# Up and gate projections turned to activations-stationary, with down projections in two passes and taps summed four tiles at a time

## The chip, the cores and the metric

The kernel runs on one core of a Trainium2 chip. The metric is the device time of one execution in microseconds (us); lower is better. Engines are named TensorE (PE, its weight loads PEld), VectorE (DVE), ScalarE (ACT), GpSimd (POOL) and SyncE (SP, which issues most DMAs). Each engine works off its own instructions in the order in which they were written out; engines wait for each other by semaphores.

## The reference

Two post-norm layers over 256 positions of width 2048, in float32. The first layer mixes with a gated MLP over windows of 128 positions, the second with latent attention; each mixer is followed by a gated MLP with a causal convolution of width 3.

```python
def gmlp_mixer(x, w_in, ln_g, ln_b, w_s, b_s, w_out):
    z = jax.nn.gelu(x @ w_in)                 # 2048 -> 2 x 6144
    u, v = jnp.split(z, 2, axis=-1)
    v = layer_norm(v, ln_g, ln_b)
    ...
    s = jnp.einsum('gij,bnjgd->bnigd', w, v) + ...   # 8 groups, masked 128x128
    return (u * s.reshape(B, S, GM_HALF)) @ w_out

def conv_ffn(x, w_up, conv_w, conv_b, w_down):
    h = x @ w_up                              # 2048 -> 2 x 5504
    h = lax.conv_general_dilated(h, ...) + conv_b    # 3 taps along the positions, per channel
    a, g = jnp.split(h, 2, axis=-1)
    return (jax.nn.silu(g) * a) @ w_down

for i in range(DEPTH):
    m = gmlp_mixer(...) if i % 2 == 0 else mla_mixer(...)
    x = layer_norm(ALPHA * x + m, ...)
    f = conv_ffn(x, ...)
    x = layer_norm(ALPHA * x + f, ...)
```

## The kernel before

Every float32 product is made from rounded halves: an operand is split into `hi` (rounded to the type float32r) and `lo` (the rest), and hi x hi, hi x lo and lo x hi are accumulated. The split of a weight load is a cast on ScalarE (`wh<-raw`) and a subtraction on VectorE (`wl<-raw,wh`).

`Feed` (line 48) walks through all weights in the order of use, as loads of 128 x 2048 (1 MB) by SyncE. `next` hands out one load and sees that two more are split and another two loaded; a load is split in two halves of 1024 columns. All tiles of this size come from one pool, `big`.

There are two forms of product. `prod_b` (line 185) holds a 128 x 128 block of activations stationary in TensorE and streams 512 weight columns: 6 matmuls of 512 for each block of 128 rows and 512 columns of weights (3 products, 2 blocks of positions). The output has positions on the partitions. `prod_a` (line 196) holds a 128 x 128 block of weights and streams the activations, `hi` and `lo` side by side: a pair of matmuls of 512 and 256 columns. The output has channels on the partitions, and its two halves have to be added (`sum_halves`).

The stages in order: `v` (prod_b, 6 groups of 1024 columns), `u` (prod_a, 12 groups of 4 tiles, each tile followed by `gate`), `wo` (`down`, prod_b), boundary with the layer norm and the first 512 columns of the up projection (`upf`), `up` (prod_a, groups 1 to 21; each pair of tiles goes through `conv` and Silu in `pair`), `dn` (`down`), boundary (`mq`), latent attention (`mq`, `mkv`, `qr`, `qn`, `kn`, `sc`, `vv`, `mo`), boundary, the second `up` and `dn`, final norm.

`down` (line 217) keeps all 8 PSUM banks: 4 pieces of 512 columns for 2 blocks of positions, one load of weights (128 x 2048) a step. The last `SKEW` steps are held back and worked off piece by piece in `boundary`, so that the norm can begin. The residual stays in two tiles of `big`.

A scheduler sets the order on each engine when the kernel is built; what stands in the code is the order in which it takes the instructions up, and an instruction whose operands it holds ready may stand earlier.

Of the kernel before, what the change touches and what calls it, by code (L numbers as in the profile page):

```python
# [15 lines left out]
P = 128  # L16
# [19 lines left out]

# [6 lines left out]


SKEW = 3


class Feed:

    def __init__(self, nc, pool, chunks):
        self.nc, self.pool, self.chunks = nc, pool, chunks
        self.raw, self.parts = {}, {}
        self.loaded = self.split = self.used = 0

    def _load(self):
        ap, cols = self.chunks[self.loaded]
        t = self.pool.tile([P, 2048], F32, tag="big", name=f"raw{self.loaded}")
        step = 512 if self.loaded == 0 else cols  # L60
        for o in range(0, cols, step):
            self.nc.sync.dma_start(t[:, o : o + step], ap[:, o : o + step])
        self.raw[self.loaded] = t
        self.loaded += 1

    def _split(self):
        i = self.split
        cols = self.chunks[i][1]
        raw = self.raw.pop(i)
        hi = self.pool.tile([P, 2048], F32R, tag="big", name=f"wh{i}")  # L70
        lo = self.pool.tile([P, 2048], F32R, tag="big", name=f"wl{i}")
        step = 512 if i == 0 else 1024 if cols == 2048 else cols // 2
        for o in range(0, cols, step):
            c = slice(o, o + step)
            self.nc.scalar.copy(hi[:, c], raw[:, c])  # L75
            self.nc.vector.tensor_tensor(lo[:, c], raw[:, c], hi[:, c].bitcast(F32), ALU.subtract)  # L76
        self.parts[i] = (hi, lo)
        self.split += 1

    def ahead(self, n_load, n_split):  # L80
        while self.split < min(n_split, len(self.chunks)):
            if self.loaded == self.split:
                self._load()
            self._split()
        while self.loaded < min(n_load, len(self.chunks)):
            self._load()

    def next(self, splits=2, loads=2):
        i = self.used
        self.ahead(i + 1 + splits + loads, i + 1 + splits)  # L90
        self.used += 1
        return self.parts.pop(i)
# [3 lines left out]
def trunk(ctx: ExitStack, tc: tile.TileContext, x, xT, gm_in, gm_wout, ffn_up, ffn_dn,  # L96
# [4 lines left out]
    big = ctx.enter_context(tc.tile_pool(name="big", bufs=22))  # L101
    tp = ctx.enter_context(tc.tile_pool(name="tp", bufs=3))
    st = ctx.enter_context(tc.tile_pool(name="st", bufs=4))
    ps = ctx.enter_context(tc.tile_pool(name="ps", bufs=8, space=bass.MemoryType.PSUM))
# [32 lines left out]
    xhl = [slot([P, 4, 512], f"xhl0_{q}", F32R) for q in range(4)]  # L137
    for j in range(4):
        t = slot([P, 4, S], f"xraw{j}")
        parts = [slice(q, q + 1) for q in range(4)] if j == 0 else [slice(0, 2), slice(2, 4)]  # L140
# [39 lines left out]

# [14 lines left out]

# [5 lines left out]
    def sum_halves(acc, name):  # L201
        lo = tp.tile([P, S], F32, tag="t1", name=f"lo_{name}", bufs=8)
        nc.scalar.copy(lo, acc[:, S : 2 * S])
        h = tp.tile([P, S], F32, tag="t1", name=f"h_{name}", bufs=8)
        nc.vector.tensor_tensor(h, acc[:, 0:S], lo, ALU.add)
        return h

    def split_act(src, name):

        t = tp.tile([P, 2 * S], F32R, tag="t2", name=name, bufs=6)  # L210
        nc.scalar.copy(t[:, 0:S], src)
        nc.vector.tensor_tensor(t[:, S : 2 * S], src, t[:, 0:S].bitcast(F32), ALU.subtract)
        return t

    full = [(f * 512, 512) for f in range(4)]

    def down(n_k, get_src, tag, ln, skew=SKEW):

        acc = [[bank(f"{tag}_{b}_{f}") for f in range(4)] for b in range(2)]
        late = []  # L220
        a = {}
        for k in range(n_k):
            for j in range(k, min(k + 2, n_k)):
                if j not in a:
                    a[j] = split_act(get_src(j), f"{tag}a{j}")
            left = n_k - 1 - k
            hi, lo = feed.next(splits=2 if left > 8 else 3 if left > 3 else 4, loads=2 if left > 3 else 1)
            if left == 6:
                ln.prep()
            t = a.pop(k)  # L230
            if left < skew:
                late.append((t, hi, lo, k))
                continue
            for b in range(2):
                prod_b(acc[b], (t[:, b * P : (b + 1) * P], t[:, S + b * P : S + (b + 1) * P]),
# [614 lines left out]
```

## Time and profile before

| | |
|---|---|
| Median of 3 runs | 2559.76 us (2559.61 to 2564.33) |
| Span of the profiled execution | 2559.8 us (its own time is not given apart from the span; the median lies within 0.1 us of it) |
| Instructions | 32217, of which matmuls 13041 |
| Stage `v` | to 272.7 us |
| Stage `u` | 272.7 to 562.3 us |
| Stage `wo` | 562.3 to 825.0 us |
| First `up` | 849.7 to 1313.6 us |
| First `dn` | 1313.6 to 1549.2 us |
| Second `up` | 1851.2 to 2315.2 us |
| Second `dn` | from 2315.2 us; the last matmul begins at 2548.9 us |

Spans go from the first to the last instruction. A row of a group reads: line, engine, operation, output and inputs by name, shapes, count, then busy time in us, mean time of one in ns, idle time of the engine before it and who ended that. Matmul times overlap: a matmul of 512 columns has a duration of 0.39 us, while the next begins much earlier; so a rate is read from a stretch of time and the number of matmuls in it.

### The profile page before, as it was taken

How to read it: one execution, taken by the hardware profiler on the slowest of the kernel's cores; microseconds unless marked ns; L12 is line 12 of the kernel's file. 1: busy time of each engine (PE TensorE's matmuls, PEld its weight loads, DVE VectorE, ACT ScalarE, POOL GpSimd, SP SyncE). 2: the span in 40 equal slices, each digit the busy share in tenths (PEclk: the TensorE clock that was granted, in tenths of full speed). 3: DMA queues.
4: the chain of work that ended last, by engine and by line, in shares of the span. 5: the costliest groups of instructions: out<-in, count | busy, mean ns of one | idle time of the engine just before them, and what ended most of it. 6: DMA issues, size and time to landing. Idle time of an engine off the chain costs nothing.

```text
span 2559.8 us, 32217 instructions
## 1 busy us (share of the span) xinstructions
PE 2544.2 (99%) x13041; PEld 2152.4 (84%) x13041; DVE 1573.6 (61%) x2284; ACT 1226.4 (48%) x1795; POOL 2.4 (0%) x15
## 2 busy tenths in 40 slices
PE   9999999999999999999999999999999999999998
PEld 7888888888888888888888888877888888888886
DVE  6444675575546766665675547845676576667554
ACT  5434444455443555544554433544365455446441
POOL 0000000000000000000000000000000000000000
PEclk9999999999999999999999999999999999999999
DMA  8545454556563545544565554424555454446552
GB/s 323 194 165 197 165 181 165 181 211 230 200 231 148 214 173 188 182 171 175 198 222 205 205 203 159 165 99 154 191 198 181 163 199 174 184 169 242 206 205 87
DMA packets 68838, 480.18 MB, mean 188 GB/s; under 512 B 7633, under 2 KB 8273, under 8 KB 11729
## 3 DMA queue, kind: packets, MB, share of 16 engines
q1 hardware_dynamic: 68688, 478.13, 52.0%
q8 instruction: 102, 1.67, 0.3%
q14 instruction: 48, 0.39, 0.0%
HBM read 476.00 MB, written 2.10 MB: 187 GB/s over the span
## 4 chain that ended last, share of the span: by engine, by line
PE 99%; DVE 1%; DMA 0%; ACT 0%; issue 0%; SPq 0%; DVEq 0%; ACTq 0%
PE up L113 36%; PE dn L113 18%; PE u L113 10%; PE v L113 10%; PE wo L113 10%; PE mo L113 4%; PE upf L113 2%; PE sc L113 1%; PE mkv L113 1%; PE qn L113 1%; PE kn L113 1%; PE vv L113 1%; PE mq L113 1%; PE s L113 1%; PE qr L113 0%; PE lnt L366 0%
## 5 line engine op out<-in xcount | busy, mean ns | idle before, releaser
L76 DVE TENSOR_TENSOR wl<-raw,wh 128x1024 fp32r<-128x1024 f32 (+2 forms) x886 | 1050.6, 1214 | 473.3 <-ACT wh L75 294.1
L75 ACT CAST wh<-raw 128x1024 fp32r<-128x1024 f32 (+2 forms) x886 | 891.0, 1044 | 523.9 <-DVE wl L76 202.8
L113 PE MATMUL up<-xhl,wh 128*128 128x512 f32 x2624 | 927.5, 399 | 0.0
L113 PE MATMUL up<-xhl,wl 128*128 128x256 f32 x2624 | 737.6, 281 | 0.0
L113 PEld LDWEIGHTS up<-xhl,wh 128*128 128x128 f32 x2624 | 493.5, 188 | 122.6
L113 PEld LDWEIGHTS up<-xhl,wl 128*128 128x128 f32 x2624 | 496.5, 189 | 0.1
L113 PE MATMUL u<-xhl,wh 128*128 128x512 f32 x768 | 268.8, 397 | 0.0
L113 PE MATMUL u<-xhl,wl 128*128 128x256 f32 x768 | 212.2, 279 | 0.0
L113 PE MATMUL v<-wh,xhl 128*128 128x512 f32 x768 | 208.2, 392 | 1.8 <-ACT wh L75 1.8
L113 PE MATMUL wo<-wh,woa 128*128 128x512 f32 x768 | 194.5, 390 | 0.0
L113 PE MATMUL dn<-wh,dn1a 128*128 128x512 f32 x688 | 174.2, 389 | 0.0
L113 PE MATMUL dn<-wh,dn0a 128*128 128x512 f32 x688 | 173.5, 390 | 0.0
L113 PEld LDWEIGHTS v<-wh,xhl 128*128 128x128 f32 x768 | 145.1, 189 | 33.1 <-ACT wh L75 2.3
L113 PEld LDWEIGHTS u<-xhl,wh 128*128 128x128 f32 x768 | 143.5, 188 | 32.8
L113 PEld LDWEIGHTS wo<-wh,woa 128*128 128x128 f32 x768 | 144.1, 188 | 29.8
L113 PEld LDWEIGHTS dn<-wh,dn0a 128*128 128x128 f32 x688 | 129.1, 188 | 26.8
L113 PEld LDWEIGHTS dn<-wh,dn1a 128*128 128x128 f32 x688 | 129.1, 188 | 26.7
L113 PEld LDWEIGHTS u<-xhl,wl 128*128 128x128 f32 x768 | 144.7, 188 | 1.1
L113 PE MATMUL v<-wl,xhl 128*128 128x512 f32 x384 | 119.0, 391 | 0.0
L113 PE MATMUL wo<-wl,woa 128*128 128x512 f32 x384 | 107.0, 390 | 0.0
L113 PE MATMUL dn<-wl,dn1a 128*128 128x512 f32 x344 | 96.0, 389 | 0.0
L113 PE MATMUL dn<-wl,dn0a 128*128 128x512 f32 x344 | 95.2, 390 | 0.0
(204 smaller groups left out, 2113.5 us busy)
## 6 DMA issues: line engine op xcount, KB each, us to landing
raw<-in_ffn_up_dram SPq DMA_DIRECT2D x172, 1024.0 KB, 4.8
raw<-in_gm_in_dram SPq DMA_DIRECT2D x95, 1024.0 KB, 4.7
raw<-in_ffn_dn_dram SPq DMA_DIRECT2D x86, 1024.0 KB, 4.7
raw<-in_gm_wout_dram SPq DMA_DIRECT2D x48, 1024.0 KB, 4.8
raw<-in_ml_out_dram SPq DMA_DIRECT2D x16, 1024.0 KB, 4.8
raw<-in_ml_b_dram SPq DMA_DIRECT2D x14, 1024.0 KB, 4.9
raw<-in_ml_kv_dram SPq DMA_DIRECT2D x5, 864.0 KB, 4.7
lng<-in_ln_rows_dram SPq DMA_DIRECT2D x4, 1024.0 KB, 6.3
```

Source lines behind the costliest of these rows:

```text
L75: self.nc.scalar.copy(hi[:, c], raw[:, c])
L76: self.nc.vector.tensor_tensor(lo[:, c], raw[:, c], hi[:, c].bitcast(F32), ALU.subtract)
L113: nc.tensor.matmul(o, l, r, start=start, stop=stop, skip_group_check=True)
```

## The change

What it does:

- `u` and `up` go from `prod_a` to the form of `prod_b`. `Square` takes 1024 weight columns as 2 x 2 PSUM banks (2 blocks of positions, 2 pieces of 512), 8 loads of 24 matmuls a group. There are 6 groups of `u` (numbers 0 to 5) and 10 groups of `up` (0 to 9) in each layer, and a tail of 2 loads that keeps `prod_a`. `out` brings the four banks into SBUF on ScalarE (Gelu in `u`, a copy in `up`: `h0_1` is that of group 1 of the first layer), and TensorE transposes each 128 x 128 block (`uT`, `ht`).
- `turned` takes four transposed tiles at a time. `conv3` writes the three taps with ScalarE, 12 instructions of 256 columns (`c0` an Identity with scale and bias, `c1` and `c2` copies with a scale), and VectorE adds the shifted taps of all four in two additions. One Silu and one multiplication of 512 follow.
- `down` takes two passes over 1024 output columns each, the second in reverse order of the steps. Its activations are split four steps at a time by `split4`, in each pass. The last 3 loads of the second pass are held back.
- A load of `u`, `up`, `wo` and `dn` is two DMAs with rows of 4 KB. A load is split whole (2048 columns), not in halves. `Feed.next` counts the tiles of `big` (now 21, before 22) and stops short of `room`.
- The residual is written to DRAM after each boundary (`park`, DMAs issued by ScalarE) and read back (`residual`) before the next norm.
- `gate` becomes `gates`, two tiles at a time; its `sb` is scaled by ScalarE.

The code also has a form with 7 products for 8 blocks (`seven`). The tables that would choose it (`GROUP_V`, `GROUP_U`, `GROUP_UP`, `SEVEN_WO`, `SEVEN_DN`) name no step, so it makes no instruction.

```diff
-SKEW = 3
+BIG = 21
+LATE = 3
+MID = 4
+T2 = 4
...
     def _split(self):
...
-        step = 512 if i == 0 else 1024 if cols == 2048 else cols // 2
+        step = 512 if self.split == 0 else cols
         for o in range(0, cols, step):
             c = slice(o, o + step)
-            self.nc.scalar.copy(hi[:, c], raw[:, c])
-            self.nc.vector.tensor_tensor(lo[:, c], raw[:, c], hi[:, c].bitcast(F32), ALU.subtract)
+            nc.scalar.copy(s.hi[:, c], raw[:, c])
+            nc.vector.tensor_tensor(s.lo[:, c], raw[:, c], s.hi[:, c].bitcast(F32), ALU.subtract)
...
+    def wide(src, base, p, sv):
+        o = (p % 2) * 1024
+        return Step([(c * 1024, 1024, src[base + 4 * c + p // 2][:, o : o + 1024]) for c in range(2)], 2048,
+                    (2 * p, 2 * p + 1), False, sv)
...
+        def plain(self, s, xs, b, fs, last):
+            for j, k in enumerate(s.ks):
+                xh, xl = x_parts(xs, k, b)
+                for which, (a, w) in enumerate(((xh, s.hi), (xh, s.lo), (xl, s.hi))):
+                    for f in fs:
+                        mm(self.acc[b][f], a, w[:, s.at(j, f)], not self.begun[b][f], last and which == 2)
+                        self.begun[b][f] = True
...
+        def out(self, name, func=None):
+            z = slot([P, 4, 512], name) if self.e is None else self.e
+            for f in range(2):
+                for b in range(2):
+                    o, src = z[:, 2 * b + f], self.acc[b][f]
...
+                    if func is not None:
+                        nc.scalar.activation(o, src, func)
+                    elif self.e is None:
+                        nc.scalar.copy(o, src)
+            return z
...
-    def conv(layer, F, acc, name):
-        h = acc if acc.shape[-1] == S else sum_halves(acc, name)
-        w = C_CONV + (layer * 2 * NF_FF + F) * 4
-        c = tp.tile([P, S], F32, tag="t1", name=f"c_{name}", bufs=8)
-        nc.scalar.activation(c, h, AF.Identity, bias=cst[:, w + 3 : w + 4], scale=cst[:, w + 2 : w + 3])
-        nc.vector.scalar_tensor_tensor(c[:, 1:S], h[:, 0 : S - 1], cst[:, w + 1 : w + 2], c[:, 1:S],
-                                       ALU.mult, ALU.add)
-        nc.vector.scalar_tensor_tensor(c[:, 2:S], h[:, 0 : S - 2], cst[:, w : w + 1], c[:, 2:S],
-                                       ALU.mult, ALU.add)
-        return c
+    def conv3(layer, tiles, name):
+        n = len(tiles)
+        c = [tp.tile([P, 4, S], F32, tag="mid", name=f"c{i}_{name}", bufs=MID) for i in range(3)]
+        for i, (F, src) in enumerate(tiles):
+            w = C_CONV + (layer * 2 * NF_FF + F) * 4
+            nc.scalar.activation(c[0][:, i], src, AF.Identity, bias=cst[:, w + 3 : w + 4], scale=cst[:, w + 2 : w + 3])
+            nc.scalar.activation(c[1][:, i], src, AF.Copy, scale=cst[:, w + 1 : w + 2])
+            nc.scalar.activation(c[2][:, i], src, AF.Copy, scale=cst[:, w : w + 1])
+        y = c[0][:, 0:n]
+        nc.vector.tensor_tensor(y[:, :, 1:S], y[:, :, 1:S], c[1][:, 0:n, 0 : S - 1], ALU.add)
+        nc.vector.tensor_tensor(y[:, :, 2:S], y[:, :, 2:S], c[2][:, 0:n, 0 : S - 2], ALU.add)
+        return y
...
+        for g in range(10):
+            feed.room = BIG - 6 - len(sums) // 2 - (4 * g + 5) // 8
...
+            z = square(f"up{layer}_{g}", GROUP_UP[g], xhl, sums, f"h{layer}_{g}").out(f"h{layer}_{g}")
+            for f in range(2):
+                banks = [bank(f"ht{layer}_{g}_{f}_{i}") for i in range(2)]
+                for i in range(2):
+                    for j in range(2):
+                        for b in range(2):
+                            o = j * S + b * P
+                            q = i * 256 + j * P
+                            nc.tensor.transpose(banks[i][:, o : o + P], z[:, 2 * b + f, q : q + P], ident)
+                turned(2 + 4 * g + 2 * f, banks)
...
+        def park(self):
+            r = []
+            for b in range(2):
+                t = dram.tile([P, D], F32, name=f"parked{self.idx}_{b}")
+                nc.scalar.dma_start(t, self.res[b])
+                r.append(t)
+            return r
```

The order at three places. In the names, `wh166` is the cast half of load number 166; the loads of `up` group g in the first layer are 148 + 8g to 155 + 8g, those of the tail 228 and 229, and the down projection begins with 230.

ScalarE at the end of group 2 of `up` in the kernel before (its loads were numbered 152 to 155; `lo_0a4` empties half a bank, `c_0a4` is the Identity of `conv`):

```order
L203 COPY lo_0a4_6848<-up0_2_0_6684 128x256 [waits PE_49]
L75 CAST wh161_7010<-raw161_6936 128x1024 [waits DMAHW6_49,DVE_49]
L460 ACTIVATE c_0a4_6852<-h_0a4_6850,cst_187 128x256 [waits DVE_49]
L203 COPY lo_0g4_6856<-up0_2_2_6686 128x256 [waits PE_49]
L75 CAST wh161_7010<-raw161_6936 128x1024
L460 ACTIVATE c_0g4_6860<-h_0g4_6858,cst_187 128x256 [waits DVE_49]
L75 CAST wh162_7092<-raw162_6976 128x1024 [waits DMAHW7_49,DVE_49]
L476 ACTIVATE s0_4_6864<-c_0g4_6860 128x256 [waits DVE_49,Activation_49]
```

ScalarE after group 1 of `up` in the changed kernel, from the last cast ahead of the copies to the next one (left out are the other conv instructions; `s0_6` and `s0_8` are the Silus of the two calls of `turned`):

```order
L100 CAST wh165_6071<-raw165_6013 128x2048 [waits DMAHW6_49,DMAHW5_49,PE_49]
L410 COPY h0_1_6102<-up0_1_0_0_5850 128x512 [waits PE_49]
L410 COPY h0_1_6102<-up0_1_1_1_5853 128x512 [waits PE_49]
L701 ACTIVATE c0_0_6_6117<-ht0_1_0_0_6107,cst_177 128x256 [waits PE_49]
L702 ACTIVATE c1_0_6_6118<-ht0_1_0_0_6107,cst_177 128x256 [waits Activation_49]
L702 ACTIVATE c1_0_8_6148<-ht0_1_1_0_6137,cst_177 128x256 [waits DVE_49]
L717 ACTIVATE s0_6_6134<-c0_0_6_6117 128x512 [waits DVE_49]
L703 ACTIVATE c2_0_8_6149<-ht0_1_1_0_6137,cst_177 128x256 [waits Activation_49]
L717 ACTIVATE s0_8_6165<-c0_0_8_6147 128x512 [waits DVE_49]
L100 CAST wh166_6172<-raw166_6044 128x2048 [waits DMAHW7_49,DMAHW0_49]
```

Before, casts alternate with the small steps of the convolution. Now, after the odd groups, 24 conv instructions and two Silus stand between the casts of the second and the third load of the next group. After the even groups two casts more stand ahead of them:

```order
L410 COPY h0_2_6420<-up0_2_0_0_6168 128x512 [waits DVE_49,PE_49]
L410 COPY h0_2_6420<-up0_2_0_1_6169 128x512 [waits PE_49]
L100 CAST wh174_6489<-raw174_6362 128x2048 [waits DMAHW7_49,DMAHW0_49,DVE_49]
L410 COPY h0_2_6420<-up0_2_1_0_6170 128x512 [waits PE_49]
L410 COPY h0_2_6420<-up0_2_1_1_6171 128x512 [waits PE_49]
L100 CAST wh175_6520<-raw175_6393 128x2048 [waits DMAHW2_49,DMAHW1_49,DVE_49]
L701 ACTIVATE c0_0_10_6435<-ht0_2_0_0_6425,cst_177 128x256 [waits PE_49]
```

The third and fourth copy have moved behind a cast there, and the fourth load is cast before the first conv instruction.

TensorE at the same place, from the last matmul of group 2 (here seven matmuls of group 3 stand among the transposes; after the odd groups the 16 transposes stand together). Before, group 3 followed group 2 directly:

```order
L167 MATMUL up0_2_1_1_6171<-wh171_6327,xhl1_3_5282 128x512
L756 MATMUL ht0_2_0_0_6425<-ident_181,h0_2_6420 128x128 [waits Activation_49]
L756 MATMUL ht0_2_1_1_6456<-ident_181,h0_2_6420 128x128 [waits PE_49]
L167 MATMUL up0_3_0_0_6485<-wh172_6358,xhl1_0_5279 128x512
L167 MATMUL up0_3_0_0_6485<-wl172_6359,xhl1_0_5279 128x512 [waits DVE_49]
L756 MATMUL ht0_2_0_0_6425<-ident_181,h0_2_6420 128x128 [waits Activation_49]
L756 MATMUL ht0_2_1_0_6455<-ident_181,h0_2_6420 128x128 [waits Activation_49]
L167 MATMUL up0_3_1_0_6487<-wh172_6358,xhl1_0_5279 128x512
```

ScalarE at the end of the first `up` (`tl0_0` empties the tail's bank, `dn0a0_0` is the first cast of the down projection's activations; before, those casts stood among the casts of `up`, some groups earlier):

```order
L717 ACTIVATE s0_40_8703<-c0_0_40_8685 128x512 [waits DVE_49]
L770 COPY tl0_0_8786<-tl0_0_8706 128x256 [waits PE_49]
L100 CAST wh230_8708<-raw230_8582 128x2048 [waits DMAHW6_49,DMAHW5_49]
L770 COPY tl0_1_8789<-tl0_1_8707 128x256 [waits PE_49]
L100 CAST wh231_8747<-raw231_8613 128x2048 [waits DMAHW7_49,DMAHW0_49]
L701 ACTIVATE c0_0_t_8792<-tl0_0_8786,cst_177 128x256 [waits DVE_49]
L702 ACTIVATE c1_0_t_8793<-tl0_0_8786,cst_177 128x256 [waits Activation_49]
L703 ACTIVATE c2_0_t_8794<-tl0_0_8786,cst_177 128x256 [waits Activation_49]
L298 CAST dn0a0_0_8812<-act0_0_5526 128x4x256
```

The first activations of the down projection have moved behind the last conv chain and two casts of weights.

More of the change, by code (lines that the diff above doesn't have):

```diff
@@ L132, in trunk @@
+    steps += whole(ml_kv[5, :, 0:KVR], KVR)
+    for t in (ml_b, ml_out):
+        for i in range(t.shape[0]):
+            steps += whole(t[i])
+    steps += up_steps(1)
+    steps += back(ffn_dn[1], NF_FF, SEVEN_DN)
+    feed = Feed(nc, big, steps)
     idle = cpool.tile([P, 512], BF16, name="idle")
@@ L215, in trunk, with split4 @@
[L215 to L235, printed above, removed]
-                       hi, lo, full, k == 0, False)
+    def split4(src8, q, n, name):
+        t = slot([P, 4, 512], name, F32R)
+        t4 = t.rearrange("p (w k) c -> p w k c", k=2)
+        src = src8[:, 2 * (q % 2) : 2 * (q % 2) + 2]
+        for w, k in ((2, 2),) if n == 4 else ((n // 2, 2), (n // 2 + 1, 1)):
+            c = (slice(None), slice(0, w) if k == 2 else slice(w - 1, w), slice(0, k))
+            hi = t4[(*c, slice(0, S))]
+            nc.scalar.copy(hi, src[c])
+            nc.vector.tensor_tensor(t4[(*c, slice(S, 2 * S))], src[c], hi.bitcast(F32), ALU.subtract)
+        return t
@@ new lines, in trunk @@
+    for gi in range(6):
+        feed.room = BIG - 4 - len(seven_quads(GROUP_U)) - 7
+        gates(gi, square(f"u{gi}", GROUP_U[gi], xhl, sums, f"u{gi}"))
+    ln = Norm(0, [x[b * P : (b + 1) * P, :] for b in range(2)])
+    acc, end = down(NF_GM, pT, SEVEN_WO, "wo", ln)
+    def conv3(layer, tiles, name):
[10 more added lines that the diff above has]
+        return y
@@ new lines, in ffn @@
+        feed.room = BIG - 12
+        tail = [bank(f"tl{layer}_{f}") for f in range(2)]
+        for c in range(2):
+            hi, lo = feed.parts()
+            for j in range(8):
+                k = 8 * c + j
+                for f in range(2):
+                    o = j * 256 + f * P
+                    prod_a(tail[f], xhl, k, hi[:, o : o + P], lo[:, o : o + P], k == 0, k == KD - 1)
+        tiles = []
+        for f in range(2):
+            t = tp.tile([P, 2, S], F32, tag="t2", name=f"tl{layer}_{f}", bufs=T2)
+            nc.scalar.copy(t[:, 0], tail[f][:, S : 2 * S])
+            nc.vector.tensor_tensor(t[:, 1], tail[f][:, 0:S], t[:, 0], ALU.add)
+            tiles.append((f * NF_FF + NF_FF - 1, t[:, 1]))
@@ L516, in trunk @@
+        gated(NF_FF - 1, conv3(layer, tiles, f"{layer}_t"), 1)
+        ln = Norm(2 * layer + 1, parked, last)
+        return (ln, *down(NF_FF, act, SEVEN_DN, f"dn{layer}", ln))
+    ln, acc, end = ffn(0, ln, acc, end, False)
     cq = [slot([P, 4, 512], "cq", F32R)]
@@ L569, in after_q @@
             latent_put(b, 0, cq, C_QG)
-    boundary(ln, acc, end, range(4), "mq", after_q)
-    xhl, res = ln.new, ln.res
+    boundary(ln, acc, end, "mq", after_q)
+    xhl, parked = ln.new, ln.park()
     kvp = [(0, KVR // 2), (KVR // 2, KVR // 2)]
```

541 lines of the change are left out of this document (353 added, 188 removed).

## The prediction

> **What bounds the kernel now.** I read the page first, then who makes TensorE wait, then the busy times by stage. From the page, the engines' busy time and the shares of the chain that ended last:
>
> ```profile
> PE 2544.2 (99%) x13041; PEld 2152.4 (84%) x13041; DVE 1573.6 (61%) x2284; ACT 1226.4 (48%) x1795; POOL 2.4 (0%) x15
> PE 99%; DVE 1%; DMA 0%; ACT 0%; issue 0%; SPq 0%; DVEq 0%; ACTq 0%
> ```
>
> All waits of TensorE (total us, times, longest):
>
> ```profile
> PE v L113 <- ACT wh L75: 1.8, 1, 1.8
> PE o L113 <- ACT pts L681: 1.5, 1, 1.5
> PE warm L113 <- POOL idle L133: 1.3, 1, 1.3
> PE qn L113 <- ACT qnlo L636: 0.5, 1, 0.5
> ```
>
> TensorE waits 5.1 us in the whole program. So every matmul added or removed counts in full, and a wait that the change creates has nothing to be traded against. Busy time by stretch: steady `v` stage, `u` stage, the two `up` stages; then the 16 `s` matmuls of one group of `u` (columns: stretch, length, busy time and instructions of each engine, clock, DMA share, GB/s; the last row has PE alone):
>
> ```profile
> 50.00:250.00 200.00, 200.00 (x880) 164.97 (x879) 99.14 (x96) 85.46 (x98) 0.00 (x0) 1.00 0.54 193
> 272.70:562.30 289.60, 289.60 (x1730) 255.29 (x1728) 197.07 (x349) 136.92 (x205) 0.00 (x0) 1.00 0.51 179
> 849.70:1313.60 463.90, 463.90 (x2629) 402.49 (x2628) 305.52 (x457) 249.01 (x378) 0.00 (x0) 1.00 0.51 184
> 1851.20:2315.20 464.00, 464.00 (x2629) 402.73 (x2628) 305.58 (x457) 249.06 (x378) 0.00 (x0) 1.00 0.52 184
> 295.27:296.97 1.70, 1.70 (x16) 1.00 0.26 34
> ```
>
> The `v` stage already has the form that the change gives to `u` and `up`: activations stationary, 512 weight columns moving, 200.00/880 = 0.2273 us a matmul. A 128x128 matmul takes 1.70/16 = 0.106 us in a run of them. One pair (512 and 256 columns, weights stationary) takes (289.6 - 192 x 0.106)/768 = 0.351 us in `u` and (463.9 - 8 x 0.106)/1312 = 0.353 us in `up`.
>
> **Terms on TensorE.** Four pairs become six matmuls of 512; the same columns stream. `up`: 2560 pairs x 0.353 = 903.4 become 3840 x 0.2273 = 872.8, **-30.6 us**. `u`: 768 x 0.351 = 269.3 become 1152 x 0.2273 = 261.8, **-7.5**. New transposes: 6 x 16 in `u`, 20 x 16 in `up`, 416 x 0.106 = **+44.2**. So the work alone is +6.1 us. Down projections: as many matmuls of the same shape, 0.
>
> **Terms from waiting.** Needed are ScalarE's and VectorE's times by shape:
>
> ```profile
> L75 ACT CAST wh<-raw 128x1024 fp32r<-128x1024 f32 x870 | 878.9, 1049 | 520.4 <-DVE wl L76 202.8 <-PE dn L113 74.4 <-PE up L113 46.0
> L75 ACT CAST wh<-raw 128x512 fp32r<-128x512 f32 x4 | 2.5, 620 | 3.6 <-DMA raw<-in_gm_in_dram 3.5
> L484 ACT COPY upt<-upf 128x512 f32<-128x512 f32 x4 | 2.3, 587 | 9.1 <-PE upf L113 9.1
> L388 ACT ACTIVATE v<-v 128x512 f32<-128x512 f32 x24 | 13.1, 602 | 88.3 <-PE v L113 88.3
> L667 ACT ACTIVATE p<-sc,mx 128x256 f32<-128x256 f32 x16 | 7.5, 466 | 0.0
> L460 ACT ACTIVATE c_0a<-uph,cst 128x256 f32<-128x256 f32 x2 | 1.1, 556 | 5.3 <-PE uph L490 5.3
> L76 DVE TENSOR_TENSOR wl<-raw,wh 128x1024 fp32r<-128x1024 f32 x870 | 1036.8, 1220 | 468.3 <-ACT wh L75 289.2 <-issue 147.8 <-PE dn L113 12.4
> L76 DVE TENSOR_TENSOR wl<-raw,wh 128x512 fp32r<-128x512 f32 x4 | 2.7, 692 | 3.6 <-ACT wh L75 3.6
> L435 DVE SCALAR_TENSOR_TENSOR sg<-s,cst,sb 128x128 f32<-128x128 f32 x96 | 28.9, 343 | 4.7 <-PE s L113 4.7
> ```
>
> How ScalarE's instructions follow each other, from the timeline (start, us):
>
> ```profile
> 859.44 0.42 ACT L476 ACTIVATE s<-c_0g 128x256 f32<-128x256 f32 x1
> 859.76 0.55 ACT L460 ACTIVATE c_0a<-uph,cst 128x256 f32<-128x256 f32 x1
> 860.21 0.55 ACT L460 ACTIVATE c_0g<-uph,cst 128x256 f32<-128x256 f32 x1
> 860.66 1.04 ACT L75 CAST wh<-raw 128x1024 fp32r<-128x1024 f32 x1
> ```
>
> A successor starts 0.1 us before the end: the 0.55 us Identity costs 0.45. Estimates from these rows: a cast of 2048 columns 1.05 + 2 x 0.43 = 1.9 us, its subtraction on VectorE 1.22 + 2 x 0.53 = 2.28. The new Copy with one column as scale is nearest to the Exp with one column as bias, 0.466, so 0.37 in a chain. One call of `turned` is then 4 x 0.45 + 8 x 0.37 = 4.8 us on ScalarE, two additions of about 1.2 us on VectorE, Silu of 512 about 0.55.
>
> Let T be the moment at which the last matmul of a group has been issued. Then 16 transposes, which need the group's four copies. One load's work (24 matmuls) lasts 24 x 0.2273 = 5.45 us.
>
> *Odd groups of `up` (1, 3, 5, 7).* The first two copies run before T; the last two end at about T+1.1, and the transposes end at T+1.9: 0.2 us lost. The order on ScalarE puts both `turned` calls and both Silus ahead of the next cast (wh166 after group 1). Chain: 1.1, 24 conv instructions 9.6, Silus 1.1, waits for the additions 0.4 (the rest under four conv instructions) and 2.2, cast 1.85: wh166 at T+16.25, wl166 at T+18.55. Two loads are ready ahead, so TensorE wants wh166 at T+1.9+10.9 = T+12.8; it waits 3.45 us, issues four matmuls (0.9), waits 1.4 for wl166. Loss 4.85 us. Then ScalarE's queue holds casts alone and is ahead again within two loads.
>
> After such a wait the clock falls, as at the start of this trace (first row: idle before it in brackets; then stretches with PE busy time and clock):
>
> ```profile
> 8.23 0.51 PE L113 MATMUL v<-wh,xhl 128*128 128x512 f32 x1 [1.81 <-ACT wh L75]
> 6.06:9.47 3.41, 1.60 (x7) 1.00 0.87 316
> 9.48:12.88 3.40, 3.40 (x9) 0.50 1.01 410
> 12.90:16.30 3.40, 3.40 (x16) 1.00 1.05 432
> ```
>
> A stretch of 3.41 us with 1.60 busy is followed by 3.40 us at half clock, 9 matmuls instead of 16: (16 - 9) x 0.227 = 1.6 us. I add it at odd groups. Together 8 x (0.2 + 4.85 + 1.6) = **+53.2**. The Trainium skill (TensorE: Matmul & The Clock Gate, section on the HAM clock gate) has the clock halved after an idle window of about 3.4 us. By that a wait of 3.45 us would seldom fill an aligned window, and the sum would be 12.8 us less; this trace disagrees, since 1.81 us of idle time were enough.
>
> *Even groups.* A cast (wh174) stands between the second and third copy, so the third ends at about T+1.9. But the order puts seven matmuls of the next group between the first four and the other transposes: TensorE gets there at T+0.4+1.6 = T+2.0. 10 x 0.2 = **+2**. Four loads are ready here, so the conv chain is covered.
>
> *`u` groups.* The same cast, and no matmuls in between; then the next group's PSUM banks wait for VectorE: two scale-adds (0.45 each, from the `sg` row), a subtraction that starts when that cast is done, a multiplication, two scale-adds, an addition, a multiplication: 1.6 + 2.28 + 0.6 + 0.85 + 0.35 + 0.6 = T+6.3, where TensorE alone would be at T+4.8. 4 x 1.5 + 2 x 1 (first and last, where the cast is missing or short) = **+8**.
>
> *End of `up`.* After group 9 the two tail loads run 32 x 0.353 = 11.3 us, to T+13.2. On ScalarE stand the conv chain (T+14.3), a copy, cast 230, a copy, cast 231, three tail conv instructions and only then the first activations of the down projection: 14.3 + 0.3 + 1.8 + 0.3 + 1.8 + 1.2 + 1.05 = T+20.8. Loss 7.6, 0.4 for VectorE's part, 0.2, and the clock 1.6: 2 x 9.8 = **+19.6**.
>
> *The rest.* The first `turned` of each layer delays a cast by about 1 us (0 to 4), start-up waits for a whole cast instead of its half (1 to 2): **+4**. At nothing: parking the residual (six writes, six reads of 1 MB), as the DMA share is 0.51 to 0.54; its reload in the attention layer stands ahead of subtractions on VectorE's queue and could cost up to 8 us once. The activations' second split in the down projections lies under 5.45 us a load, of which VectorE needs 2.3. Two DMAs a load instead of one on SP's queue also cost nothing while loads run two ahead; now 1 MB in rows of 8 KB lands in 4.8 us, and the one load with rows of 2.25 KB in 3.6:
>
> ```profile
> raw<-in_ffn_up_dram SPq DMA_DIRECT2D x172, 1024.0 KB, 4.8
> raw<-in_ml_kv_dram SPq DMA_DIRECT2D x1, 288.0 KB, 3.6
> ```
>
> Sum: 6.1 + 53.2 + 2 + 8 + 19.6 + 4 = +92.9. The profiled execution has a span of 2559.8 us, and the median of the runs is 2559.76, so nothing has to be added around it: 2559.8 + 92.9 = **2653 us**.
>
> **Rivals.**
> 1. *The casts come in time.* If the conv instructions overlap more, or wait less for VectorE, wh166 is there before T+12.8 and the odd groups lose 0.2 us each: 2653 - 51.6 = 2601 us. It needs 3.5 us off a 15 us chain for the cast, and 4.9 for the subtraction. Against it: Identity is measured at 0.45 in a chain, and the last additions cannot overlap anything. 0.13.
> 2. *The chain is longer.* If the conv instructions don't overlap and Copy costs 0.56 as Identity does, a chain grows by 24 x 0.14 = 3.4 us; it stands in ten places: +34, and +3 to +8 from the reload: about 2692 us. For it: the scale comes from a column for each. 0.15.
> 3. *Loads become the bound.* Rows of 4 KB instead of 8 KB: if a row took as long as now, the DMA share 0.54 would be 1.08, and a load 5.9 us instead of 5.45. With 344 such loads (48, 48, 160, 88): +155, 2808 us. Against it: the short rows of the second line above land early. 0.03.
> 4. *Faster.* The transposes pay only below 38.1/416 = 0.092 us each with every wait covered. At 0.08 us, and if ScalarE had its copies ready at once and its casts early: 2559.8 - 38.1 + 33.3 = 2555 us. Against it: 0.106 is measured back to back, and ScalarE's order is fixed. 0.02. Between (transposes near 0.092, waits covered): 0.04 for no change.
>
> **Numbers.** The forecast (2630 to 2680) has 0.63. The range takes in rivals 1 and 2: 2598 to 2710. A measurement of this kernel can tell about 0.2% (5 us) from no change. Faster 0.02, same 0.04, slower 0.94.
>
> **What would show it.** In the profile after: `up` and `u` matmuls at 0.227 us; 416 transposes near 0.106; TensorE waiting about 39 us in `up` for ScalarE's `wh` and VectorE's `wl`, in eight places, each followed by 3.4 us at half clock; two waits of about 8 us for the first `dn` activations; ScalarE busy for (8 x 1.9 + 9.6 + 1.1 + 4 x 0.5) = 28 us of a group of some 48. Wrong it would be if ScalarE's conv instructions are far from 0.37 to 0.45 us, if a cast in front of the copies starts late, or if the clock stays up.

## The result, and the profile after

The changed kernel takes 2654.11 us (median of four runs, 2652.7 to 2658.5) against 2559.69 us before: a ratio of 1.0366, 95% interval 1.0351 to 1.0381. The profiled execution has a span of 2651.6 us, 91.8 us more than before. The forecast was 2653. Each ratio below is to runs of the kernel before that were made along with the version's own, and their median is not always 2559.69: it was 2566.29 us for experiments 1 to 4, 2559.5 for 5, 6 and the first two of 7, and 2565.23 for the last two, with single runs from 2559.0 to 2569.1.

From the page after, the engines' busy time and the chain that ended last:

```profile
PE 2581.9 (97%) x11793; PEld 2126.3 (80%) x11793; DVE 1428.0 (54%) x1167; ACT 1282.7 (48%) x1478; POOL 2.4 (0%) x15
PE 90%; ACT 4%; DVE 4%; issue 0%; DMA 0%; SPq 0%; DVEq 0%; ACTq 0%
```

ScalarE and VectorE have become 8% of the chain. TensorE's waits (total us, times, longest), the first four of the list:

```profile
PE up L167 <- ACT wh L100: 29.8, 8, 4.0
PE dn L167 <- ACT dn0a L298: 8.1, 1, 8.1
PE dn L167 <- ACT dn1a L298: 8.1, 1, 8.1
PE up L167 <- DVE wl L101: 5.4, 10, 0.9
```

Before, all waits together were 5.1 us. These four lines hold 51.4: eight waits in `up` and one at each way into a down projection. The stages, from their first matmul to that of the next one: `u`, then `up` of either layer (columns as in the stretches before the change):

```profile
274.26:568.16 293.90, 293.88 (x1442) 247.95 (x1440) 159.75 (x156) 124.16 (x124) 0.00 (x0) 1.00 0.50 176
855.37:1360.98 505.61, 479.57 (x2150) 393.05 (x2148) 249.13 (x146) 288.77 (x404) 0.00 (x0) 0.97 0.49 170
1901.83:2405.55 503.72, 478.35 (x2149) 392.21 (x2147) 248.99 (x146) 288.75 (x404) 0.00 (x0) 0.97 0.50 171
```

`up` was 464.0 us and its clock 1.00. Now TensorE is idle for 25 to 26 us of either `up` stage, and the clock is 0.97. ScalarE is busy for 28.9 us a group, as the forecast's 28. The same reading for every kernel of this study, in us, worked out from the first matmul of each stage in its trace (the waits ahead of `dn` lie in `up`; `dn` 1 ends where `mkv` begins, `dn` 2 with the span):

| Stage | before | after | defer | tail | one tap less | both | no turns |
|---|---|---|---|---|---|---|---|
| `v` | 267.0 | 268.6 | 267.6 | 268.3 | 268.5 | 268.5 | 268.2 |
| `u` | 289.6 | 293.9 | 293.9 | 293.9 | 293.9 | 293.9 | 293.9 |
| `wo` to `up` 1 | 287.4 | 287.2 | 287.2 | 287.2 | 287.2 | 287.2 | 287.2 |
| `up` 1 | 464.0 | 505.6 | 474.5 | 497.7 | 471.7 | 466.2 | 448.1 |
| `dn` 1 | 260.2 | 261.5 | 262.6 | 259.9 | 261.5 | 259.9 | 260.0 |
| `mkv` to `up` 2 | 277.4 | 279.3 | 279.5 | 279.4 | 279.5 | 279.5 | 279.5 |
| `up` 2 | 464.0 | 503.7 | 474.5 | 498.3 | 471.6 | 466.2 | 448.1 |
| `dn` 2 | 244.6 | 246.1 | 247.4 | 244.5 | 246.4 | 244.6 | 244.6 |

Of the 91.8 us, 81.3 lie in the two `up` stages, 4.3 in `u`, 2.8 in the down projections, 1.6 in `v` and 2.0 between `mkv` and the second `up`; the stretch from `wo` to the first `up` is 0.2 shorter.

One of the eight waits, after group 1. TensorE's rows (start, duration, idle time before it in brackets; the 16 transposes first), then ScalarE's: the last copies, the last conv instruction, the Silu and the casts:

```profile
945.85 2.14 PE L756 MATMUL ht<-ident,h 128*128 128x128 f32 x16
...
957.84 0.62 PE L167 MATMUL up<-wl,xhl 128*128 128x512 f32 x2
958.30 0.61 PE L167 MATMUL up<-wh,xhl 128*128 128x512 f32 x2
962.94 2.08 PE L167 MATMUL up<-wh,xhl 128*128 128x512 f32 x4 [4.03 <-ACT wh L100]
965.27 1.22 PE L167 MATMUL up<-wl,xhl 128*128 128x512 f32 x2 [0.25 <-DVE wl L101]
```

```profile
945.82 1.07 ACT L410 COPY h<-up 128x512 f32<-128x512 f32 x2 [0.28 <-PE up L167]
957.36 0.52 ACT L703 ACTIVATE c<-ht,cst 128x256 f32<-128x256 f32 x1
960.47 0.63 ACT L717 ACTIVATE s<-c 128x512 f32<-128x512 f32 x1 [2.59 <-DVE c L706]
961.01 9.10 ACT L100 CAST wh<-raw 128x2048 fp32r<-128x2048 f32 x5
```

The transposes begin at 945.85, which is the forecast's T. The first cast after the chain ends at 961.01 + 1.9 = 962.9 = T+17.1 (forecast 16.25), and TensorE has run dry at 958.9 = T+13.1 (forecast 12.8). ScalarE itself waited 2.6 us for VectorE's additions with five casts queued behind.

The clock around this wait, in stretches of 3.41 us:

```profile
958.02:961.43 3.41, 0.89 (x4) 0.39 (x3) 2.26 (x3) 0.96 (x2) 0.00 (x0) 1.00 0.47 154
961.43:964.84 3.41, 1.90 (x4) 1.17 (x4) 2.31 (x2) 3.41 (x3) 0.00 (x0) 0.50 0.42 156
964.84:968.26 3.42, 3.17 (x8) 2.42 (x8) 3.42 (x3) 3.42 (x3) 0.00 (x0) 0.50 0.00 0
968.26:971.67 3.41, 3.41 (x16) 2.80 (x16) 3.41 (x2) 2.44 (x3) 0.00 (x0) 1.00 0.93 357
```

A stretch with 0.89 us of work is followed by two at half clock, not one; so it is in seven of the eight places. TensorE works for 5.07 us in them at half speed: 2.5 us lost, where the forecast had 1.6. From the first matmul of group 2 to the transposes behind its last (947.74 to 998.53) pass 50.8 us for 192 matmuls that need 192 x 0.2268 = 43.5: 7.2 us lost.

### The profile page after: what moved, and what is told of

The parts are those of the page before. It is cut to its first block, busy times and chain, and to the rows that moved or that the text cites. A ratio compares the mean times of both kernels' runs of the same rounds, so it can differ in the third digit from the quotient of the medians.

```text
span 2651.6 us, 29004 instructions
## 1 busy us (share of the span) xinstructions
PE 2581.9 (97%) x11793; PEld 2126.3 (80%) x11793; DVE 1428.0 (54%) x1167; ACT 1282.7 (48%) x1478; POOL 2.4 (0%) x15
## 4 chain that ended last, share of the span: by engine, by line
PE 90%; ACT 4%; DVE 4%; issue 0%; DMA 0%; SPq 0%; DVEq 0%; ACTq 0%
PE up L167 30%; PE dn L167 17%; PE u L167 10%; PE wo L167 10%; PE v L167 10%; PE mo L167 3%; PE upf L167 2%; PE sc L167 1%; DVE wl L101 1%; PE ht L756 1%; ACT c L701 1%; ACT wh L100 1%; PE mkv L167 1%; DVE c L705 1%; DVE c L706 1%; ACT c L702 1%
## 5 line engine op out<-in xcount | busy, mean ns | idle before, releaser
L101 DVE TENSOR_TENSOR wl<-raw,wh 128x2048 fp32r<-128x2048 f32 (+1 forms) x447 | 1001.3, 2258 | 594.2 <-ACT wh L100 447.7
L100 ACT CAST wh<-raw 128x2048 fp32r<-128x2048 f32 (+1 forms) x447 | 839.0, 1907 | 498.8 <-DVE wl L101 143.1
L167 PE MATMUL up<-wh,xhl 128*128 128x512 f32 x2560 | 707.8, 396 | 29.8 <-ACT wh L100 29.8
L167 PEld LDWEIGHTS up<-wh,xhl 128*128 128x128 f32 x2560 | 486.3, 191 | 134.0 <-ACT wh L100 33.2
L167 PE MATMUL up<-wl,xhl 128*128 128x512 f32 x1280 | 403.8, 397 | 5.4 <-DVE wl L101 5.4
L167 PEld LDWEIGHTS up<-wl,xhl 128*128 128x128 f32 x1280 | 244.2, 192 | 62.9 <-DVE wl L101 11.9
L167 PE MATMUL u<-wh,xhl 128*128 128x512 f32 x768 | 206.7, 390 | 0.0
L705 DVE TENSOR_TENSOR c<-c,c 128x1020 f32<-128x1020 f32 x42 | 51.3, 1222 | 267.9 <-ACT c L702 267.9
L167 PEld LDWEIGHTS u<-wh,xhl 128*128 128x128 f32 x768 | 143.8, 188 | 29.6
L167 PE MATMUL u<-wl,xhl 128*128 128x512 f32 x384 | 118.4, 389 | 0.0
```

The source lines that it names most:

```text
L100: nc.scalar.copy(s.hi[:, c], raw[:, c])
L101: nc.vector.tensor_tensor(s.lo[:, c], raw[:, c], s.hi[:, c].bitcast(F32), ALU.subtract)
L167: nc.tensor.matmul(o, l, r, start=start, stop=stop, skip_group_check=True)
L705: nc.vector.tensor_tensor(y[:, :, 1:S], y[:, :, 1:S], c[1][:, 0:n, 0 : S - 1], ALU.add)
```

## The experiments

**1. Casts ahead of the conv chain (defer).** The two `turned` calls of a group wait in a list and are issued inside the next group.

```diff
     def square(tag, order, xs, sums, name, late=()):
...
             sq.step(s, xs, sums, i == len(order) - 1)
+            if late and i in (1, 3):
+                late.pop(0)()
...
-                turned(2 + 4 * g + 2 * f, banks)
+                if g < 9:
+                    late.append(lambda a=2 + 4 * g + 2 * f, banks=banks: turned(a, banks))
+                else:
+                    turned(2 + 4 * g + 2 * f, banks)
```

> The changed kernel with one thing moved: the two `turned` calls of a group of `up` (0 to 8) are issued after the second and the fourth load of the next group, so that ScalarE has four loads cast ahead when the conv instructions begin, and casts stand between them. Nothing is left out. Theory A (the odd groups lose because the casts stand behind the whole conv chain): in the changed kernel an odd group and what follows cost 50.8 us for 192 matmuls that need 43.5, so 7.2 us are lost in each of eight places, 35.2 us of it waits of `up` for `wh` and `wl`. These go below 5 us in all, the eight half-clock stretches go, and an odd group keeps some 0.3 us: 8 x 6.9 = 55 us less, 2654 - 55 = 2599 us. Theory B (ScalarE, VectorE or the loads cannot keep up with an odd group, whatever the order): the wait moves to another load, 2640 to 2654 us. Theory C (the half clock comes from something else than the waits, such as the transposes): the waits go and the half clock stays, 8 x 4.3 less, 2620 us.

Measured: 2595.27 us (2594.06 to 2596.66), 1.0115 of before (1.0094 to 1.0135). Its casts after group 1 on ScalarE, two ahead of the chain and two within it, and the only wait of `up` that is left:

```profile
944.29 1.91 ACT L100 CAST wh<-raw 128x2048 fp32r<-128x2048 f32 x1
947.05 1.94 ACT L100 CAST wh<-raw 128x2048 fp32r<-128x2048 f32 x1
953.50 2.03 ACT L100 CAST wh<-raw 128x2048 fp32r<-128x2048 f32 x1
956.51 1.90 ACT L100 CAST wh<-raw 128x2048 fp32r<-128x2048 f32 x1
```

```profile
PE up L167 <- DVE wl L101: 1.6, 2, 0.8
```

ScalarE and VectorE do the same work; only the order differs. The eight waits and the half-clock stretches behind them are gone, and either `up` stage is 29 to 31 us shorter. Theory A holds; B and C fall. So the loss of the odd groups is the order on ScalarE (VectorE's additions move along with it), and the half clock follows from the waits.

**2. The way into the down projection (tail).** The deferring of experiment 1 for group 9 alone (into the two tail loads), and the first two `dn` activations split ahead of it; in group 9, room is kept for two tiles more:

```diff
-            feed.room = BIG - 6 - len(sums) // 2 - (4 * g + 5) // 8
+            feed.room = BIG - 6 - len(sums) // 2 - (4 * g + 5) // 8 - (2 if g == 9 else 0)
+            if g == 9:
+                first = {q: split4(act[0], q, 4, f"dn{layer}a0_{q}") for q in range(2)}
...
-        return (ln, *down(NF_FF, act, SEVEN_DN, f"dn{layer}", ln))
+        return (ln, *down(NF_FF, act, SEVEN_DN, f"dn{layer}", ln, first))
```

> The changed kernel with only the end of each `up` stage changed: the first two `dn` activations are split ahead of group 9, and the two `turned` calls of group 9 are issued after the first and the second of the two tail loads. Nothing is left out. Theory A (the first `dn` matmul waits because the split of its activations stands behind the conv chain, two casts and the tail's conv): both waits of 8.1 us go, with the half clock that follows in `dn` (about 1.5 us each): 2 x 9.6 = 19 us less, 2635 us. Theory B (behind that wait stands another, for the casts and subtractions of the first two `dn` loads): half of it stays as a wait for `wh` or `wl`, 2644 us. Theory C (VectorE or the loads set the start of `dn`): 2650 to 2654 us.

Measured: 2637.31 us (2634.05 to 2638.8), 1.0276 of before (1.0257 to 1.0294). No wait for `dn0a` or `dn1a` is left, and none came in its place at the start of `dn`. The `up` stages are 7.9 and 5.4 us shorter, the `dn` stages 1.6 each. The second `up` gains less because here all eight odd-group waits are followed by two half-clock stretches. Theory A holds. Which of the two moves takes the wait away is not separated.

**3. A shorter chain in the same order (one tap less).** The third tap is left out, so the values are not those of the reference.

```diff
-            nc.scalar.activation(c[2][:, i], src, AF.Copy, scale=cst[:, w : w + 1])
...
-        nc.vector.tensor_tensor(y[:, :, 2:S], y[:, :, 2:S], c[2][:, 0:n, 0 : S - 2], ALU.add)
```

> The changed kernel without the third tap of the convolution: the Copy of the third tap (four in each call of `conv3`) and its addition are left out; the order of the rest is that of the changed kernel. The chain on ScalarE behind an odd group gets shorter by 8 x 0.36 = 2.9 us and by one addition that it waits for, 1.3 us: the cast that came 17.1 us after the last matmul of the group should come at 12.9, just when TensorE wants it (12.9), and its subtraction at 15.2, 1.4 us after TensorE wants that (13.8). Theory A (the chain's length sets the wait, microsecond for microsecond): TensorE's waits in `up` fall from 35.2 us to about 11, all for VectorE's `wl`; the two waits for `dn` fall from 8.1 to about 4. If 1.4 us of idle time do not lower the clock, an odd group loses 1.6 instead of 7.2, and the time is 2654 - 45 - 8 = 2601 us; if they do, it is about 2621. Theory B (something else than the chain makes the odd groups wait): the waits stay, and the time is above 2640 us.

Measured: 2586.84 us (2586.7 to 2587.71), 1.0081 of before (1.0065 to 1.0098). Its waits of TensorE for the two disputed places, then the transposes after group 1, and the casts behind its chain:

```profile
PE up L167 <- DVE wl L101: 4.2, 8, 0.5
PE dn L167 <- ACT dn0a L298: 2.2, 1, 2.2
PE dn L167 <- ACT dn1a L298: 2.2, 1, 2.2
```

```profile
944.50 2.14 PE L754 MATMUL ht<-ident,h 128*128 128x128 f32 x16
```

```profile
954.71 10.94 ACT L100 CAST wh<-raw 128x2048 fp32r<-128x2048 f32 x6
```

Here T is 944.50. The first cast ends at 954.71 + 1.9 = T+12.1 and not at T+12.9, so the wait that is left is 0.5 us and not 1.4, and the clock stays up in `up`. Of the 14 us between 2601 and the measurement, eight waits 0.9 us shorter are 7 and the two of `dn` 1.8 shorter are 4; the other 3 were not followed. The chain's length sets the wait, and the waits of eight places are eight equal ones. Theory A holds, its size was short.

**4. Both moves (both).** The edits of 1 and 2 together, `turned` of every group deferred.

> Both moves together: `turned` of every group is issued after the second and the fourth load of the next group (of group 9 after the tail's loads), and the first two `dn` activations are split ahead of group 9. Nothing is left out. Theory A (the two waits are the whole loss beside the work on TensorE): both savings add up, 55 + 19 = 74 us less, 2580 us, no half clock between the start and the end, and 20 us more than before the change: 6 from TensorE's own work, the rest in small pieces at the ends of groups. Theory D (with the waits gone the new form of the products is faster than the old one, and the time falls below that before the change): under 2555 us. Theory B (a shared limit of ScalarE, VectorE or loads shows once the first waits are gone): above 2600 us.

Measured: 2573.54 us (2572.2 to 2576.43), 1.0032 of before (1.0022 to 1.0042). The two `up` stages:

```profile
855.20:1321.39 466.19, 465.37 (x2150) 386.25 (x2148) 247.38 (x144) 283.69 (x394) 0.00 (x0) 1.00 0.53 184
1860.77:2326.92 466.15, 465.33 (x2150) 386.26 (x2148) 247.38 (x144) 283.66 (x394) 0.00 (x0) 1.00 0.53 183
```

TensorE is busy for all but 0.8 us of them at full clock. So 2651.6 - 2571.5 = 80.1 us of the change's 91.8 were waits, with the clock that they cost. The stages, in which a single wait of 0.8 us is left, are still 2.2 us longer than the 464.0 before. Theory A holds, though it saved 6 us more than the 74 it had forecast; B and D fall.

**5. Without the transposes (no turns).** In the version of 4 the conv instructions read the copies as they lie:

```diff
-                            nc.tensor.transpose(banks[i][:, o : o + P], z[:, 2 * b + f, q : q + P], ident)
+                banks = [z[:, 2 * i + f] for i in range(2)]
```

> The version with both moves, without the 320 transposes of `up`: the conv instructions read the copies `h` as they lie (tokens on partitions) in place of the transposed tiles, so the activations that go on are not those of the reference. The copies stay. Theory A (the new form of the products saves TensorE's time, and the transposes take more than that back): 320 x 0.109 = 34.9 us less than with them, 2573.5 - 34.9 = 2539 us, each `up` stage 466.2 - 17.4 = 449 us, 15 us under the 464.0 before the change, and the whole 20 us faster than before the change. Theory E (the transposes lie beside other work, such as the wait for the copies or for free banks, and cost TensorE little): 2563 us or more.

Measured: 2536.49 us (2536.17 to 2536.83), 0.9905 of before (0.9888 to 0.9923). Its first `up` stage:

```profile
854.57:1302.64 448.07, 447.25 (x1989) 370.41 (x1988) 245.81 (x143) 288.83 (x390) 0.00 (x0) 1.00 0.56 189
```

160 transposes are 466.19 - 448.07 = 18.1 us, 0.113 each, and nothing hides them. The new form of the products saves 464.0 - 448.1 = 15.9 us a stage. Theory A holds: the form is faster, and its transposes cost more than it saves.

**6. Halves for seven loads (halves).**

```diff
-        step = 512 if self.split == 0 else cols
+        step = 512 if self.split == 0 else 1024 if self.split in (1, 2, 3, 314, 315, 316, 317) else cols
```

The text of its expectation says eleven loads; the edit halves seven, those named in it.

> The version with both moves, with the casts and subtractions of eleven loads in two halves of 1024 columns as before the change: the first four loads of `v` (the first of them was in parts already) and the four loads of `upf` of the second layer. Nothing is left out. Theory A (the 1.5 us that `v` takes longer than before the change, and the 2.5 us of the stretch from `mo` to `up` of the second layer, in which `upf` waits 1.9 us for VectorE's `xhl`, come from subtractions of a whole load, 2.28 us, that others stand behind): both go for the most part, 2 to 4 us less, 2570 to 2571 us. Theory F (the late reload of the parked residual, or the second split of the activations, makes these waits): `v` loses its 1.5 us, `mo` to `up` stays at 156.4 us, 2572 us.

Measured: 2570.42 us (2570.25 to 2570.76), 1.0038 of before (1.0023 to 1.0053). `v` takes 265.9 us, 2.6 less than with whole loads. The stretch from `mkv` to the second `up` goes from 279.5 to 279.0 only; the wait of `upf` is gone, and another stands a little ahead of it:

```profile
PE lnt L614 <- DVE res L603: 1.6, 1, 1.6
```

So the start of `v` is A's, and the time lies in A's range although only one of its two savings came. At the second boundary the size of the subtraction is not what counts. There the chain that ended last goes through two of VectorE's whole subtractions in the changed kernel (2.28 and 2.20 us, among the steps of the layer norm) and through two pairs of halves here (2.36 and 2.27 us), since the halves of a load stand back to back; before the change it goes through TensorE alone. No instruction waits for the reload of the residual. No run moves these subtractions, so that their place costs the 2 us is read from the chain and not shown by an experiment.

**7. Seven products for eight (seven, seven_v_u, seven_up, seven_down).** The code's own unused form, switched on by its tables, as a way to a version faster than both. It takes 21 matmuls for 24.

```diff
-GROUP_V = [NONE] * 6
-GROUP_U = [NONE] * 6
-GROUP_UP = [NONE] * 10
+GROUP_V = [TWO] * 6
+GROUP_U = [TWO] * 6
+GROUP_UP = [TWO] * 10
```

> The version with both moves, with the seven-product path that the code holds switched on (the table TWO in place of NONE) for two of eight loads in every group of `v`, `u` and `up`. Nothing is left out. Such a load needs 21 matmuls of 512 columns in place of 24, so 64 loads save 192 x 0.227 = 43.6 us on TensorE, for one more cast of 2048 columns on ScalarE (1.9 us) and sums and a subtraction on VectorE (about 5 us) each. Theory A (TensorE is the bound again once the two moves are made, and the others have room: VectorE works 243 us of 497 in an `up` stage): 2530 us, 30 us faster than before the change. Theory B (VectorE's longer order delays subtractions, and new waits and half-clock stretches take it back): 2560 us or more.

> As the run with seven products in every group of `v`, `u` and `up`, but with `up` left at eight products: 24 loads save 72 x 0.227 = 16.3 us. Theory A: 2573.5 - 16.3 = 2557 us. Theory B (the sums of the activations, which VectorE makes at the start, and its longer order delay the first groups): 2565 us or more.

Measured: 2574.73 us (1.0055 of before, 1.0040 to 1.0070) and 2579.16 (1.0072, 1.0057 to 1.0087); by the time, B holds for both. In the first, the combined loads wait for VectorE, the mean clock is 0.993 and not 0.998, and the largest waits are:

```profile
PE u L167 <- DVE wl L101: 5.6, 1, 5.6
PE up_p L167 <- DVE tl L105: 4.5, 4, 1.1
PE ht L761 <- DVE h L405: 4.2, 4, 1.8
```

An `up` stage takes 465 us, 1 less than without, though 13.6 us of matmuls are gone. The same tables, with THREE in `up` alone, and with four steps of every half of the down projections (`SEVEN_WO = SEVEN_DN = (16, 20, 32, 36)`):

> The version with both moves and the halved casts, with seven products for three of eight loads in every group of `up` alone (the table THREE), 60 loads, 180 x 0.227 = 40.9 us less on TensorE. Nothing is left out. With two such loads a group an `up` stage took 465.1 us in place of 466.2, though 13.6 us of matmuls were gone: some 12.5 us went into waits. Theory A (most of those 12.5 us stand once in a group, at the first combined load and ahead of the transposes, whose copies became additions on VectorE): the third load saves its 0.68 us in each group, an `up` stage takes 458 us, and the time is 2554 us. Theory B (every such load waits for VectorE by itself): 2568 us or more.

> The version with both moves and the halved casts, with seven products in place of eight for the loads that begin at k = 16, 20, 32 and 36 of every half of the three down projections (24 loads); `v`, `u` and `up` stay at eight products. Nothing is left out. 24 x 3 matmuls fewer save 72 x 0.227 = 16.3 us. Theory A (VectorE has room in the down projections, where there are no taps and no copies: 2570.4 - 16.3 = 2554 us, which is 0.2% under the time before the change). Theory B (as in the runs with seven products in `v`, `u` and `up`, a new wait for VectorE's subtraction of the combined weights stands at each such load, about 1 us, and the sums at the end of a half delay the layer norm): 2570 us or more.

Measured: `seven_up` 2602.76 us (1.0151, 1.0134 to 1.0168). By the time, B holds, but the largest of its new waits is for ScalarE's casts and not for VectorE:

```profile
PE up L167 <- ACT wh L100: 14.2, 18, 2.6
PE up L167 <- DVE wl L101: 9.9, 10, 2.0
PE ht L761 <- DVE h L405: 8.2, 12, 2.4
```

`seven_down`, the fastest whole version: 2560.81 us (2559.03 to 2561.6), 0.9989 of before (0.9979 to 0.9998), which is no difference that this measurement can tell; the runs of the kernel before that belong to it spread from 2559.15 to 2569.12 us. The time lies between the two theories (2554, and 2570 or more). Against experiment 6, the second `dn` is 5.4 us shorter, all that its matmuls save; `wo` and the first `dn` are only 3.1 shorter. Most of the other 2.3 stands in new waits behind these two, 1.6 us and 0.2 us each, of the next projection for the layer norm's output, as the last clause of B has it:

```profile
PE upf L167 <- DVE xhl L618: 1.6, 1, 1.6
PE mq L167 <- DVE xhl L618: 1.6, 1, 1.6
```

No version that computes everything beats the kernel before by more than the 0.2%.

## Why the prediction was right, by its own steps

**The form of the products** (-30.6 in `up`, -7.5 in `u`): experiment 5 shows -15.9 a stage, -31.9 in `up`. Right. The -7.5 of `u` has no run of its own.

**The transposes** (+44.2): in `up` 36.2 instead of 320 x 0.106 = 33.9, as one costs 0.113 with its edges. Right, and the bound given in the rival for a gain (0.092 us each) is the reason that the version without waits is still slower. In a run, start to start is 0.109. The Trainium skill (TensorE: Matmul & The Clock Gate, section on LDWEIGHTS) gives a weight load as its columns over 1.2 GHz, an estimate of 107 ns for 128 columns, which agrees with 0.109. The profile counts a weight load for every matmul (11793 of each), but no run separates the load from the rest of a transpose, so that it sets the price is not shown.

**The odd groups** (+53.2): the mechanism is shown by experiments 1 and 3. Their size was 60.3 us (505.6 - 474.5 and 503.7 - 474.5), with the edges of the even groups in it. In the rows after group 1 the conv instructions follow each other as forecast: an Identity takes 0.45 us from start to start and a Copy 0.36. The waits were 35.2 us instead of 38.8: the cast came 0.8 us later than computed, but the four matmuls that it lets go ran at half clock and took 2.1 us instead of 0.9, so that only 0.25 (0.25 to 0.9 in the eight places) was left to wait for the subtraction instead of 1.4. The step that was too small is the clock's: 1.6 us for one stretch at half clock, where the trace has two, 2.5 us. Why a second one follows stays open: in the seven places the first half-clock stretch holds 1.9 to 3.15 us of work, and in the eighth, behind which the clock is full again, 2.94.

**Rival 1** (the casts come in time, 2601 us) is what experiment 1 makes: 2595. It needed another order, not a shorter chain. **Rival 2** (a longer chain) falls with the 0.45 and 0.36; its 3.4 us should by its own figures have been 24 x 0.56 - 9.6 = 3.8. **Rival 3** (loads) falls as well: the two DMAs of a load land in 4.3 to 4.5 us, and TensorE waits for none.

**End of `up`** (+19.6): experiment 2 gives 16.8 from the medians; from `defer` to `both`, which differ in this alone, 21.7; of the 80.1 that both moves take away, the odd groups' 60.3 leave 19.8. The waits were 8.1 each (7.6 forecast); the three figures differ as the waits lie differently on the stretches of the clock.

**Even groups and first `turned`** (+2, +2): no run changes the even groups alone, as experiment 1 moves their chains too. In the trace of the changed kernel an odd group, from its first matmul to the next group's, holds 12 transposes of the even group ahead and its own 16, and takes 46.9 us. 192 matmuls (43.52 in `no turns`) and 28 transposes of 0.114 make 46.7, so 0.2 us are lost at the edges of two groups, where the forecast had 0.2 for each. These are part of the 60.3. The first `turned` shows as the only wait of `up` that is left in `both`, 0.8 us for a subtraction in group 0 of either layer. It is in `no turns` too, so it lies inside the 448.1, and the form saves 0.8 a stage more than the 15.9.

**`u`** (+8): measured 293.9 - (289.6 - 7.5 + 10.2) = 1.6. This step failed. The rows after group 1 of `u`, in which T is 366.80:

```profile
366.80 0.27 PE L668 MATMUL uT<-ident,u 128*128 128x128 f32 x1
...
371.75 0.61 PE L167 MATMUL s<-wT,v 128*128 128x128 f32 x4
372.12 0.70 PE L167 MATMUL u<-wh,xhl 128*128 128x512 f32 x2
372.71 0.68 DVE L684 TENSOR_TENSOR v<-uT,sg 128x512 f32<-128x512 f32 x1
```

VectorE ends that multiplication at T+6.6, close to the T+6.3 of the forecast. But the next group's first matmul starts at T+5.3, ahead of it: the bank that this multiplication frees is not among those that are wanted first. And TensorE alone needs 48 x 0.109 = 5.2, not 4.8 (with the forecast's own 0.106 it is 5.1).

**The rest**: start-up 1.6 (1 to 2 forecast), and 2.0 between `mkv` and the second `up`, for which the sum had nothing. The forecast named the reload there; the chain goes through whole subtractions instead (experiment 6). Down projections 0 beside the clock after their wait, but for 0.3 less in the first; no wait shows for parking.

So it is partly luck that the sum came out near 92: 5 us too few for odd and even groups and 2 too few for the transposes stood against 6 too many for `u` and 3 too many for the form with the first calls. The measured terms are -39.4 + 46.4 + 60.3 + 19.8 + 1.6 + 3.3 - 0.2 = 91.8, where 3.3 is 1.6 + 2.0 - 0.3 of the rest. By the medians the change costs 94.4 us and not 91.8: a run's time is some 2 us above its span (2653.4 and 2651.6 for the profiled run after), so the profiled execution before, with a span of 2559.8, was itself slower than the median of 2559.69, and the forecast's reading that nothing has to be added around the span was wrong.

## What to carry to other kernels

Turning a product so that the long side streams can save a few per cent of its matmul time, but a result that then has to be transposed pays for each 128x128 block, 0.113 us here; compare the two sums before building it. On an engine that works in order, take the time from the end of a group to the next cast and set it against the loads that are ready ahead; moving the group's closing work two and four loads into the next group cost nothing here and gave back 59 us. A wait of TensorE of 2 us or more can cost more than its length: count the half-clock time behind it, too.

## What was not expected of the hardware

**How little idle time lowers the clock.** Stretches of 3.41 us on the grid of the clock's changes. Two of the version with one tap less; full clock follows the first, half clock the second:

```profile
1842.07:1845.48 3.41, 1.89 (x8) 1.58 (x9) 3.41 (x6) 0.23 (x1) 0.00 (x0) 1.00 0.64 251
1323.25:1326.66 3.41, 1.39 (x9) 0.94 (x7) 3.12 (x2) 3.41 (x5) 0.00 (x0) 1.00 0.32 80
```

The start of the version with both moves, with the stretch that follows:

```profile
12.94:16.35 3.41, 1.69 (x6) 1.12 (x7) 2.84 (x3) 1.59 (x3) 0.53 (x1) 1.00 1.04 433
16.35:19.76 3.41, 3.41 (x10) 2.63 (x9) 0.77 (x3) 1.90 (x1) 0.00 (x0) 0.50 1.01 414
```

One of the version `tail`, which full clock follows:

```profile
1865.70:1869.11 3.41, 1.58 (x7) 1.32 (x8) 3.41 (x5) 0.55 (x1) 0.00 (x0) 1.00 0.73 271
```

From full clock, in the traces of the two kernels and of experiments 1 to 4, it stayed up after every stretch with 1.89 us of work or more, and halved after each with 1.69 or less but for this last row. So in these traces about half a stretch decides, and a wait of some 2 us can already be dear if it lies within one stretch, while 0.5 us (experiment 3) costs itself alone. The Trainium skill (TensorE: Matmul & The Clock Gate, section on the HAM clock gate) speaks of an idle window of about 3.4 us; here half of one was enough.

**A transpose hides its price in the next matmul.** In the version with both moves, four transposes, and then two rows of matmuls:

```profile
945.68 0.60 PE L761 MATMUL ht<-ident,h 128*128 128x128 f32 x4
946.04 0.71 PE L167 MATMUL up<-wh,xhl 128*128 128x512 f32 x2
946.58 0.62 PE L167 MATMUL up<-wl,xhl 128*128 128x512 f32 x2
```

The first 512-matmul starts 0.36 us after the first of four transposes (three at 0.109 and one at 0.03), and the two matmuls then take 0.54 instead of 0.45. The last transpose seems almost free and is paid behind it.
